# Seven block products for eight in a feed-forward of two inputs, and a modulation that is computed earlier

## The chip, the cores and the metric

The kernel runs on one core of a Trainium2 chip. The metric is the device time of one execution in microseconds, the median of several runs. Everything is float32 at the outside; the large matmuls run as three products of operands that are split in a rounded high part and a low remainder.

## What is computed

`x` is a sequence of 256 tokens of 1024 channels, `ctx` a context of 256 tokens. A first block (mixer and feed-forward) runs on `x`; then come two layers on `x` and `ctx` together, whose shifts, scales and gates come from a modulation, a matrix product of a condition vector. Cut to what the change touches:

```python
def swiglu(h, w_in, w_out):
    g, u = jnp.split(h @ w_in, 2, axis=-1)
    return (jax.nn.silu(g) * u) @ w_out

for l in range(2):
    with_ctx = l < 1
    mod = (silu_c @ w_mod[l] + b_mod[l])[:, None, :]
    mod_c = (silu_cc @ w_mod[l] + b_mod[l])[None, None, :]
    ...
    y, yc = even_mixer(h, hc, ...) if l % 2 == 0 else odd_mixer(h, hc, ...)
    x = x + gt_m * rmsnorm(y, g_post_mix[l])
    h = modulate(x, g_pre_ffn[l], sh_f, sc_f)
    x = x + gt_f * rmsnorm(swiglu(h, w_ffn_in[l], w_ffn_out[l]), g_post_ffn[l])
    if with_ctx:
        ctx = ctx + cgt_m * rmsnorm(yc, g_post_mix[l])
        hc = modulate(ctx, g_pre_ffn[l], csh_f, csc_f)
        ctx = ctx + cgt_f * rmsnorm(swiglu(hc, w_ffn_in[l], w_ffn_out[l]), g_post_ffn[l])
```

The hidden width is 2816, 22 blocks of 128. Only layer 0 has a feed-forward of both inputs.

## The kernel before

**Stages.** One program runs straight through, by the profiled execution: the first block's mixer (0 to 345 us), its feed-forward (345 to 566), layer 0's mixing (566 to 701), a boundary and block 0 of the feed-forward (701 to 728), layer 0's feed-forward (to 1030), layer 1's attention (to 1260) and its feed-forward (to 1457).

**Weights.** `wraw` (L173) loads a raw weight tile over the SP queue, in one of 3 buffers of 128x1024 ("m", 512 KB) or 4 of 128x512 ("f", 256 KB). `wload` (L178) splits it with `split` (L313): ScalarE rounds the high part (L314), VectorE subtracts for the low one (L315). `prod_w1` (L208) multiplies 128 weight columns with an input of 256 tokens: for each of 8 pieces of the 1024 channels three matmuls, high by high, high by low, low by high (L215 to L217). `mm_x` (L226, L227 to L229) is the same with tokens as the stationary side.

**Feed-forward.** `ffn_main` (L419) goes over 22 hidden blocks. With a second input (`more`, the context in `ch`, `cl`) a block has 4 products of 24 matmuls of 128x256: gate and up of each input, 96 in all. `swiglu` (L413) needs a tanh on ScalarE and two operations on VectorE per input. The latent's hidden block is split and goes one block later through `Down.step` (L290), 12 matmuls of 128x512; the context's is kept in `hid` for a later stage.

**Boundary.** `boundary` (L390) closes a stage: it adds the result to `x`, normalizes two tiles of 128 tokens (`rstd_of` L318, whose power runs on GpSimd, L331), transposes them (L346) and splits them. Between the two tiles `fill` may put other matmuls; ahead of layer 0's feed-forward that is `ctx_first` (L1266), gate and up of the context for block 0.

**Modulation.** `modulation(l, ...)` (L501) is a generator: three parts `b` of two halves `h` of eight raw tiles `wraw` of 512 KB. A raw goes either through TensorE, four float32 matmuls against `sst` (`rows`, L528), or through VectorE into an accumulator, two operations a raw (L548, L550), which at the end of a half are picked into rows by TensorE. Layer 0's modulation runs in the first block. Layer 1's is started with layer 0's feed-forward: its first half on TensorE, the other five on VectorE.

**Order.** A generator handed to `side.start` is stepped whenever `tick` has gathered so many estimated microseconds of matmul work; `side.finish` runs it to its end. Within these hints a scheduler sets the final order of each engine's instructions. An engine and a queue work their list strictly in that order. The context's projections and attention (`ctx_project`, L1202) are such a side work of the first block's feed-forward; `down_f` (L1177) multiplies the context's attention result `cah`, `cal` with the output matrix in 96 matmuls of 128x512, and its place in the order is the scheduler's.

## Time and profile before

| what | value |
|---|---|
| median of 3 runs | 1454.36 us (1453.89 to 1455.94) |
| the profiled execution | 1459.17 us, its span 1457.4 us |
| mean granted clock of TensorE | 0.978 of full speed |
| TensorE busy | 1393.5 us, 96% |
| VectorE busy | 982.7 us, 67% |
| ScalarE busy | 717.7 us, 49% |
| GpSimd busy | 37.8 us, 3% |

Busy is the union of an engine's instructions. Matmuls overlap: a matmul's duration holds its way through the array, so what one costs in a row of them is the distance from start to start. A wait's releaser is inferred. PE is TensorE, DVE is VectorE, ACT is ScalarE, POOL is GpSimd, SP is the engine that issues most transfers.

### The profile page before, as it was taken

How to read it: one execution, taken by the hardware profiler on the slowest of the kernel's cores; microseconds unless marked ns; L12 is line 12 of the kernel's file. 1: busy time of each engine (PE TensorE's matmuls, PEld its weight loads, DVE VectorE, ACT ScalarE, POOL GpSimd, SP SyncE). 2: the span in 40 equal slices, each digit the busy share in tenths (PEclk: the TensorE clock that was granted, in tenths of full speed). 3: DMA queues.
4: the chain of work that ended last, by engine and by line, in shares of the span. 5: the costliest groups of instructions: out<-in, count | busy, mean ns of one | idle time of the engine just before them, and what ended most of it. 6: DMA issues, size and time to landing. Idle time of an engine off the chain costs nothing.

```text
span 1457.4 us, 25376 instructions
## 1 busy us (share of the span) xinstructions
PE 1393.5 (96%) x9900; PEld 1233.2 (85%) x9900; DVE 982.7 (67%) x1949; ACT 717.7 (49%) x1326; POOL 37.8 (3%) x58
## 2 busy tenths in 40 slices
PE   6999999999999998989899999999899999899997
PEld 5887879978999986877699999999778866799997
DVE  4877954576667656776686768664688886455555
ACT  4467743455554545557523232222577676344443
POOL 1000000000000000001000000000000000000000
PEclk8999999999999999989999999999999999899999
DMA  7763799857566552622875656543374511256663
GB/s 249 226 183 88 227 281 281 240 166 218 171 181 197 164 151 81 206 94 67 248 224 178 211 169 200 182 145 102 104 229 150 176 45 30 73 160 188 189 187 117
DMA packets 294464, 246.87 MB, mean 169 GB/s; under 512 B 11380, under 2 KB 273144, under 8 KB 294344
## 3 DMA queue, kind: packets, MB, share of 16 engines
q1 hardware_dynamic: 294344, 245.25, 55.1%
q8 instruction: 78, 1.28, 0.4%
q14 instruction: 42, 0.34, 0.1%
HBM read 244.13 MB, written 1.08 MB: 168 GB/s over the span
## 4 chain that ended last, share of the span: by engine, by line
PE 82%; DVE 7%; ACT 4%; DMA 3%; issue 2%; POOL 1%; SPq 0%; POOLq 0%; DVEq 0%; ACTq 0%
PE pb L215 14%; PE pb L216 14%; PE pb L217 14%; PE pb L227 9%; PE pb L228 9%; PE pb L229 9%; PE pb L1052 2%; PE pb L528 2%; PE pb L1004 2%; PE pb L1046 1%; DVE mlo L315 1%; DMA mraw<-in_w_in_dram 1%; ACT mhi L314 1%; DMA wraw<-in_w_mod_dram 1%; PE pb L772 1%
## 5 line engine op out<-in xcount | busy, mean ns | idle before, releaser
L315 DVE TENSOR_TENSOR mlo<-mraw,mhi 128x1024 fp32r<-128x1024 f32 (+2 forms) x297 | 360.8, 1218 | 279.1 <-ACT mhi L314 269.8
L314 ACT ACTIVATE mhi<-mraw 128x1024 fp32r<-128x1024 f32 (+2 forms) x297 | 311.8, 1054 | 426.7 <-PE pb L216 227.5
L215 PE MATMUL pb<-xTh,mhi 128*128 128x256 f32 x1632 | 466.2, 286 | 1.2 <-DVE ge L861 0.7
L217 PE MATMUL pb<-xTh,mlo 128*128 128x256 f32 x1632 | 464.3, 285 | 1.3 <-DVE mlo L315 1.3
L216 PE MATMUL pb<-xTl,mhi 128*128 128x256 f32 x1632 | 464.8, 285 | 0.0
L215 PEld LDWEIGHTS pb<-xTh,mhi 128*128 128x128 f32 x1632 | 314.0, 192 | 12.2 <-issue 6.1
L217 PEld LDWEIGHTS pb<-xTh,mlo 128*128 128x128 f32 x1632 | 314.0, 192 | 3.9 <-DVE mlo L315 2.0
L216 PEld LDWEIGHTS pb<-xTl,mhi 128*128 128x128 f32 x1632 | 314.2, 193 | 3.4 <-DVE xTl L315 0.8
L227 PE MATMUL pb<-mhi,fh 128*128 128x512 f32 x264 | 104.2, 395 | 0.0
L228 PE MATMUL pb<-mlo,fh 128*128 128x512 f32 x264 | 103.7, 393 | 0.0
L229 PE MATMUL pb<-mhi,fl 128*128 128x512 f32 x264 | 103.0, 390 | 0.0
L550 DVE SCALAR_TENSOR_TENSOR acc<-wraw,sst,acc 128x1024 f32<-128x1024 f32 x70 | 86.9, 1280 | 6.0 <-DMA wraw<-in_w_mod_dram 5.6
L227 PE MATMUL pb<-mhi,xTh 128*128 128x256 f32 (+1 forms) x272 | 81.0, 298 | 4.1 <-ACT xTh L314 2.5
L228 PE MATMUL pb<-mlo,xTh 128*128 128x256 f32 (+1 forms) x272 | 81.4, 299 | 1.8 <-DVE mlo L315 1.8
L229 PE MATMUL pb<-mhi,xTl 128*128 128x256 f32 (+1 forms) x272 | 80.9, 297 | 0.4 <-DVE xTl L315 0.4
L315 DVE TENSOR_TENSOR flo<-fraw,fhi 128x512 fp32r<-128x512 f32 x88 | 59.9, 688 | 12.6 <-ACT fhi L314 10.7
L314 ACT ACTIVATE fhi<-fraw 128x512 fp32r<-128x512 f32 x88 | 54.5, 625 | 17.7 <-PE pb L229 9.2
L227 PEld LDWEIGHTS pb<-mhi,xTh 128*128 128x128 f32 x272 | 54.3, 200 | 7.6 <-ACT xTh L314 2.9
L229 PEld LDWEIGHTS pb<-mhi,fl 128*128 128x128 f32 x264 | 49.6, 188 | 10.8 <-DVE fl L315 0.3
L228 PEld LDWEIGHTS pb<-mlo,xTh 128*128 128x128 f32 x272 | 54.4, 200 | 4.9 <-DVE mlo L315 2.6
L227 PEld LDWEIGHTS pb<-mhi,fh 128*128 128x128 f32 x264 | 49.8, 189 | 10.1 <-issue 0.8
L228 PEld LDWEIGHTS pb<-mlo,fh 128*128 128x128 f32 x264 | 49.8, 189 | 8.8 <-issue 0.8
(402 smaller groups left out, 2339.2 us busy)
## 6 DMA issues: line engine op xcount, KB each, us to landing
...
```

The costliest lines, as they stand in the source:

```text
L215: nc.tensor.matmul(dst, wh, xh[:, k], start=(k == 0), stop=False)
L216: nc.tensor.matmul(dst, wh, xl[:, k], start=False, stop=False)
L217: ins = nc.tensor.matmul(dst, wl, xh[:, k], start=False, stop=(k == 7))
L227: nc.tensor.matmul(dst, xh_k, wh, start=first, stop=False)
L228: nc.tensor.matmul(dst, xh_k, wl, start=False, stop=False)
L229: return nc.tensor.matmul(dst, xl_k, wh, start=False, stop=last)
L314: return (nc.scalar.activation(hi, src, AF.Copy), nc.vector.tensor_sub(lo, src, hi.bitcast(F32)))
L315: nc.vector.tensor_sub(lo, src, hi.bitcast(F32)))
L528: ins = nc.tensor.matmul(pb[32 * q:32 * q + 32, h * 256:(h + 1) * 256], lhs, rhs[:, q], start=first, stop=last, tile_position=(0, 32 * q), ...
L550: ins = nc.vector.scalar_tensor_tensor(acc[:, r_], raw, col, acc[:, r_], OP.mult, OP.add)
L1004: nc.tensor.matmul(sb[j][:, n * S:(n + 1) * S], qs[a][hd, i * P:(i + 1) * P], keys[n][b][hd, kv, :], start=(m == 0), stop=(m == 2))
L1052: nc.tensor.matmul(ob[64 * j:64 * j + 64, :S], vals[k // 2](k % 2, kv), pts[j][:, k], start=(k == 0), stop=(k == 2 * nb - 1), skip_group_c ...
```

## The change

**The products.** In blocks 1 to 21 of layer 0's feed-forward the gate matrix and the up matrix are taken as halves by input channel (`g0`, `g1`, `u0`, `u1`, each 4 pieces of 128x128) and the two inputs likewise (`x0`, `x1` and the context's). The four results, gate and up of both inputs, come from seven half products of 12 matmuls of 128x256, 84 for 96. For this GpSimd makes four sums of 128x512 of the raw weights per block (`s1`, `s2`, `u0` in place, `s4`); each of the seven halves is split by itself; ScalarE copies one product out of PSUM (`e1`) and VectorE makes five sums of products. The sums take slots of the "f" raw pool. Sums of the inputs (`t1` to `t4`) are made once around the boundary by `sums_of_inputs`, partly on GpSimd. Block 0 stays as it was.

**The modulation of layer 1.** Part `b` = 0 runs wholly on VectorE beside the first block's feed-forward, as a second side work (`side2`) that starts once the context's projections have begun. Parts 1 and 2 run wholly on TensorE during layer 0's mixing: 32 raws in pairs, with two buffers (`nraw` 2, `step` 2), all done before layer 0's feed-forward. In the feed-forward itself nothing of it is left.

```diff
...
+        lo, hi = slice(0, 4), slice(4, 8)
+        f = lambda a: a.bitcast(F32)
+        t3 = mp.tile([P, 4, S], F32, tag="mP", name="t3", bufs=2)
+        nc.vector.tensor_sub(t3, f(ch[:, hi]), f(ch[:, lo]))
+        u = mp.tile([P, 4, S], F32, tag="mP", name="u3", bufs=2)
+        nc.vector.tensor_sub(u, f(cl[:, hi]), f(cl[:, lo]))
+        nc.vector.tensor_add(t3, t3, u)
+        split(*rooms[2], t3)
+        yield
+        t2 = t3
+        nc.vector.tensor_add(t2, t3, keep[0])
+        split(*rooms[1], t2)
+        nc.gpsimd.tensor_tensor(u, f(ch[:, lo]), keep[0], op=OP.subtract)
+        nc.gpsimd.tensor_tensor(u, u, f(cl[:, lo]), op=OP.add)
+        nc.gpsimd.tensor_tensor(keep[1], keep[1], t2, op=OP.subtract)
+        split(*rooms[0], u)
+        h4, l4 = rooms[3]
+        nc.scalar.activation(h4, keep[1], AF.Copy)
+        for j in range(2):
+            js = slice(2 * j, 2 * j + 2)
+            nc.vector.tensor_sub(l4[j], keep[1][:, js], h4[:, js].bitcast(F32))
...
+            def halves(s, *src):
+                hi = wpool[s].tile([P, CH[s]], F32R, tag=s + "hi", name=s + "hi", bufs=HLB[s])
+                lo = wpool[s].tile([P, CH[s]], F32R, tag=s + "lo", name=s + "lo", bufs=HLB[s])
+                res = []
+                for j, a in enumerate(src):
+                    o = slice(512 * j, 512 * j + 512)
+                    split(hi[:, o], lo[:, o], a)
+                    res.append(parts(hi[:, o].rearrange("p (a b) -> p a b", a=4),
+                                     lo[:, o].rearrange("p (a b) -> p a b", a=4)))
+                return res
+            def product(dst, w, b, fresh=True):
+                for k in range(4):
+                    (wh, wl), (bh, bl) = w[k], b[k]
+                    nc.tensor.matmul(dst, wh, bh, start=fresh and k == 0, stop=False, skip_group_check=True)
+                    nc.tensor.matmul(dst, wh, bl, start=False, stop=False, skip_group_check=True)
+                    nc.tensor.matmul(dst, wl, bh, start=False, stop=(k == 3), skip_group_check=True)
+            def swiglu2(t, g, u):
+                nc.scalar.activation(t, g, AF.Tanh, scale=0.5)
+                nc.vector.scalar_tensor_tensor(t, t, 1.0, g, OP.add, OP.mult)
+                nc.vector.tensor_mul(t, t, u)
...
+            for c in range(1, 22):
+                tick(9.1)
+                g = wraw(wview(W, 0, 8, c * P, P), 8, P, "m")
+                u = wraw(wview(W, 0, 8, 2816 + c * P, P), 8, P, "m")
+                g0, g1, u0, u1 = g[:, :512], g[:, 512:], u[:, :512], u[:, 512:]
+                s1, s2, s4 = [wpool["f"].tile([P, 512], F32, tag="fraw", name="fs", bufs=RAWB["f"])
+                              for j in range(3)]
+                nc.gpsimd.tensor_tensor(s1, u0, u1, op=OP.add)
+                nc.gpsimd.tensor_tensor(s2, s1, g0, op=OP.subtract)
+                nc.gpsimd.tensor_tensor(u0, g0, u0, op=OP.subtract)
+                nc.gpsimd.tensor_tensor(s4, g1, s2, op=OP.subtract)
+                b1, b2, b3 = [bank("MF"[(c + j) % 2])[:, :S] for j in range(3)]
+                wg0, ws2 = halves("m", g0, s2)
+                product(b1, wg0, x0)
+                product(b2, ws2, t2)
+                e1 = fp.tile([P, S], F32, tag="e1", name="e1", bufs=2)
+                nc.scalar.activation(e1, b1, AF.Copy)
+                e2 = fp.tile([P, S], F32, tag="e2", name="e2")
+                nc.vector.tensor_add(e2, b2, e1)
+                ws3, wg1 = halves("m", u0, g1)
+                product(b3, ws3, t3)
+                product(b1, wg1, x1, False)
+                ws1, = halves("f", s1)
+                product(b2, ws1, t1, False)
+                e4 = fp.tile([P, S], F32, tag="e4", name="e4")
+                nc.vector.tensor_add(e4, b2, e1)
+                nc.vector.tensor_add(e4, b3, e4)
+                dn.step(*prev)
+                wu1, = halves("f", u1)
+                product(b3, wu1, t4, False)
+                ws4, = halves("f", s4)
+                product(b2, ws4, c1, False)
+                nc.vector.tensor_add(e2, b3, e2)
+                nc.vector.tensor_add(e1, b2, e1)
+                t = fp.tile([P, S], F32, tag="ft", name="ft", bufs=2)
+                swiglu2(t, b1, e2)
+                prev = hidden(c, t)
+                swiglu2(hid[:, c], e1, e4)
...
+                if not vec:
+                    for k in range(0, 8, step):
+                        if step < 8:
+                            raws = [load(k + j) for j in range(step)]
+                            yield
+                        pb = bank("F")
+                        for j in range(step):
+                            rows(sst[:, k + j], raws[j] if step < 8 else load(k + j), j == 0, j == step - 1)
+                            if step == 8:
+                                yield
+                        add()
...
+    def second(acc):
+        while not begun:
+            yield
+        yield from modulation(1, wm, mods[1], acc, (0,))
+    side2.start(second(lambda: cp.tile([P, 2, 4, 256], F32, tag="ftmp", name="acc")), 6)
...
+    wm1 = ExitStack()
+    side.start(modulation(1, wm1.enter_context(tc.tile_pool(name="wm1", bufs=1, side="right")), mods[1],
+                          None, (1, 2), 2, 2), 4)
...
+    more = sums_of_inputs(ch, cl, keep, rooms, mp)
+    next(more)
+    xh, xl = boundary(dn.y, 1.0, gain_row(Gm, "gm0"), Af, Bf, fill=ctx_first, keep=keep)
+    rooms[1] = pair(*[ap_.tile([P, D], F32R, tag="mtmp", name="t2p", bufs=2) for j in range(2)])
+    rooms[3] = (pair(ap_.tile([P, D], F32R, tag="mG", name="t4h", bufs=1))[0],
+                [cst.tile([P, 2, S], F32R, tag="mmod", name="t4l", bufs=2) for j in range(2)])
+    next(more)
+    side.finish()
     l0.close()
+    wm1.close()
...
-    side.start(modulation(1, wm1.enter_context(tc.tile_pool(name="wm1", bufs=1, side="right")), mods[1],
-                          lambda: cp.tile([P, 2, 4, 256], F32, tag="ftmp", name="acc")), 5)
-    y = ffn_main(xh, xl, T["w_ffn_in_2"][0], 0, T["w_ffn_in_2"][0], 2816, T["w_ffn_out_2"][0],
-                 (ch, cl, hid), first)
+    y = ffn_pair(xh, xl, ch, cl, rooms, T["w_ffn_in_2"][0], T["w_ffn_out_2"][0], first, hid)
...
```

**What moves in the order.** TensorE, the boundary at the start of layer 0's mixing, while the first tile is normalized; `cah` is the context's attention result, `wraw` a raw of the modulation, `xn` the normalized tile. Before:

```order
L1052 MATMUL pb_6539<-PTm_6525,kvc_3895 64x256
L1052 MATMUL pb_6539<-PTm_6532,kvc_3895 64x256
L227 MATMUL pb_7497<-fhi_7501,cah_5646 128x512 [waits PE_49]
L228 MATMUL pb_7497<-flo_7502,cah_5646 128x512
L229 MATMUL pb_7497<-fhi_7501,cal_5647 128x512
L227 MATMUL pb_7497<-fhi_7513,cah_5646 128x512
```

After:

```order
L1202 MATMUL pb_6655<-PTm_6648,kvc_3901 64x256
L668 MATMUL pb_6896<-wraw_6809,sst_179 32x256 [waits DMAHW3_49,DMAHW4_49,DMAHW2_49,DMAHW5_49,DMAHW1_49,DMAHW7_49,DMAHW0_49,PE_49]
L668 MATMUL pb_6896<-wraw_6809,sst_179 32x256 x3
L668 MATMUL pb_6896<-wraw_6811,sst_179 32x256 [waits DMAHW4_49]
L668 MATMUL pb_6896<-wraw_6811,sst_179 32x256 x3
L668 MATMUL pb_6970<-wraw_6906,sst_179 32x256 [waits DMAHW5_49,DVE_49]
L351 MATMUL pb_6732<-tab_76,xn_6711 128x128 [waits DVE_49]
L351 MATMUL pb_6732<-tab_76,xn_6711 128x128 x3
L351 MATMUL pb_6744<-tab_76,xn_6711 128x128 x4
L668 MATMUL pb_6970<-wraw_6906,sst_179 32x256 x3
L668 MATMUL pb_6970<-wraw_6908,sst_179 32x256 [waits DMAHW6_49]
```

The context's down matmuls have left this place (they now stand from the last part of the layer's attention on); six raws of the modulation stand there, with DMA waits of their own, four of them behind or between the transposes.

TensorE, the end of layer 0's mixing; `a0h`, `a0l` is the attention result, `xTh` by `mhi` is `ctx_first`. Before:

```order
L228 MATMUL pb_7795<-mlo_7901,a0h_7124 128x512
L229 MATMUL pb_7795<-mhi_7900,a0l_7125 128x512
L215 MATMUL pb_7989<-xTh_7727,mhi_7992 128x256 [waits DVE_49,Activation_49]
L216 MATMUL pb_7989<-xTl_7728,mhi_7992 128x256 [waits DVE_49]
L217 MATMUL pb_7989<-xTh_7727,mlo_7993 128x256 [waits DVE_49]
L215 MATMUL pb_7989<-xTh_7727,mhi_7992 128x256
```

After:

```order
L233 MATMUL pb_8091<-mhi_8266,a0l_7330 128x512
L668 MATMUL pb_8092<-wraw_7784,sst_179 32x256 [waits DMAHW6_49,Activation_49]
L668 MATMUL pb_8092<-wraw_7784,sst_179 32x256 x3
L668 MATMUL pb_8092<-wraw_7786,sst_179 32x256 [waits DMAHW7_49]
L668 MATMUL pb_8092<-wraw_7786,sst_179 32x256 x3
L351 MATMUL pb_8338<-tab_76,xn_8317 128x128 [waits DVE_49]
L351 MATMUL pb_8338<-tab_76,xn_8317 128x128 x3
L351 MATMUL pb_8349<-tab_76,xn_8317 128x128 x4
L668 MATMUL pb_8142<-wraw_8102,sst_179 32x256 [waits DMAHW0_49,PE_49]
L668 MATMUL pb_8142<-wraw_8102,sst_179 32x256 x3
```

After the last down matmul two raws follow, the first tile's transposes, and then more raws (seven, in all nine ahead of `ctx_first`); before, `ctx_first` followed at once.

VectorE, one hidden block of layer 0's feed-forward. Before:

```order
L315 TENSOR_TENSOR mlo_11194<-mraw_11191,mhi_11193 128x1024 [waits DMAHW0_49,PE_49,Activation_49]
L416 SCALAR_TENSOR_TENSOR ft_11106<-ft_11106,pb_10996 128x256 [waits Activation_49]
L417 TENSOR_TENSOR ft_11106<-ft_11106,pb_10996 128x256 [waits DVE_49]
L315 TENSOR_TENSOR mlo_11259<-mraw_11256,mhi_11258 128x1024 [waits DMAHW1_49,Activation_49]
L315 TENSOR_TENSOR fl_11114<-ft_11106,fh_11113 128x256 [waits Activation_49]
L315 TENSOR_TENSOR mlo_11267<-mraw_11264,mhi_11266 128x1024 [waits DMAHW2_49,PE_49,Activation_49]
```

After (`mlo` and `flo` of 128x512 are the low parts of weight halves, `fs` a sum, `e1`, `e2`, `e4` sums of products; the last line of this piece is the split of the second up half):

```order
L319 TENSOR_TENSOR mlo_10995<-mraw_10980,mhi_10994 128x512 [waits DMAHW7_49,Activation_49]
L319 TENSOR_TENSOR mlo_10995<-fs_10985,mhi_10994 128x512 [waits Activation_49]
L319 TENSOR_TENSOR mlo_11029<-mraw_10982,mhi_11028 128x512 [waits DMAHW0_49,PE_49,Activation_49]
L535 SCALAR_TENSOR_TENSOR ft_10969<-ft_10969,pb_10831 128x256 [waits Activation_49]
L572 TENSOR_TENSOR e4_10914<-pb_10832,e1_10864 128x256 [waits DVE_49,PE_49]
L319 TENSOR_TENSOR mlo_11029<-mraw_10980,mhi_11028 128x512 [waits Activation_49]
L573 TENSOR_TENSOR e4_10914<-pb_10833,e4_10914 128x256 [waits DVE_49]
L319 TENSOR_TENSOR flo_11059<-fs_10984,fhi_11058 128x512 [waits Activation_49]
L319 TENSOR_TENSOR mlo_11080<-mraw_11077,mhi_11079 128x1024 [waits DMAHW1_49,Activation_49]
L579 TENSOR_TENSOR e2_10866<-pb_10833,e2_10866 128x256 [waits PE_49]
L319 TENSOR_TENSOR flo_11096<-mraw_10982,fhi_11095 128x512 [waits Activation_49]
L580 TENSOR_TENSOR e1_10864<-pb_10832,e1_10864 128x256 [waits PE_49]
```

Weight splits went from one tile of 1024 at a time to halves, with the sums of products between them. The raw tile read by the last line here is the up tile, whose buffer the next block's up load takes.

GpSimd, the four sums of one block, of which there were none:

```order
L554 TENSOR_TENSOR fs_10984<-mraw_10982 128x512 [waits DMAHW0_49,DVE_49]
L555 TENSOR_TENSOR fs_10985<-fs_10984,mraw_10980 128x512 [waits DMAHW7_49,DVE_49,Pool_49]
L556 TENSOR_TENSOR mraw_10982<-mraw_10980,mraw_10982 128x512 [waits DMAHW6_49,DVE_49]
L557 TENSOR_TENSOR fs_10986<-mraw_10980,fs_10985 128x512 [waits Pool_49]
```

The first waits for the up tile's load, the second for the gate tile's as well; the third writes over a half of the up tile.

## Rows read from the trace of the kernel before

**Rows 1.** Part 1 of the page: busy time, share of the span, instructions of TensorE.

```profile
PE 1393.5 (96%) x9900; PEld 1233.2 (85%) x9900; DVE 982.7 (67%) x1949; ACT 717.7 (49%) x1326; POOL 37.8 (3%) x58
```

**Rows 2.** Part 4 of the page: the chain that ended last, shares by engine.

```profile
PE 82%; DVE 7%; ACT 4%; DMA 3%; issue 2%; POOL 1%; SPq 0%; POOLq 0%; DVEq 0%; ACTq 0%
```

**Rows 3.** Windows: three stages; busy us (instructions) of each engine, granted clock, DMA share, GB/s.

```profile
345.00:560.00 215.00, 214.11 (x1523) 197.04 (x1522) 140.86 (x249) 113.45 (x199) 5.40 (x5) 1.00 0.60 180
566.30:700.80 134.50, 122.43 (x738) 98.61 (x738) 99.57 (x235) 84.00 (x175) 10.51 (x13) 0.94 0.39 121
740.00:1030.00 290.00, 290.00 (x2242) 276.41 (x2241) 194.69 (x242) 83.81 (x126) 1.06 (x2) 1.00 0.57 175
```

**Rows 4.** Timeline of ScalarE: start us, us; a tanh of two neighbouring blocks.

```profile
838.25 0.38 ACT L415 ACTIVATE hid<-pb 128x256 f32<-128x256 f32 x1 [1.89 <-PE pb L217]
852.50 0.38 ACT L415 ACTIVATE hid<-pb 128x256 f32<-128x256 f32 x1 [1.89 <-PE pb L217]
```

**Rows 5.** Timeline of TensorE: two neighbouring matmuls of each width.

```profile
689.62 0.39 PE L229 MATMUL pb<-mhi,a0l 128*128 128x512 f32 x1
689.85 0.39 PE L227 MATMUL pb<-mhi,a0h 128*128 128x512 f32 x1
...
707.95 0.28 PE L217 MATMUL pb<-xTh,mlo 128*128 128x256 f32 x1
708.07 0.28 PE L215 MATMUL pb<-xTh,mhi 128*128 128x256 f32 x1
```

**Rows 6.** The chain from 740 to 1030 us: the first of five such pieces.

```profile
766.94 1.00 PE pb L528 x16
```

**Rows 7.** Groups of VectorE by form, 740 to 1030 us: busy, mean ns, idle before.

```profile
L550 DVE SCALAR_TENSOR_TENSOR acc<-wraw,sst,acc 128x1024 f32<-128x1024 f32 x64 | 79.5, 1279 | 5.5 <-DMA wraw<-in_w_mod_dram 5.2
L315 DVE TENSOR_TENSOR mlo<-mraw,mhi 128x1024 fp32r<-128x1024 f32 x60 | 73.2, 1223 | 75.3 <-ACT mhi L314 70.0 <-PE pb L528 5.2
L417 DVE TENSOR_TENSOR hid<-hid,pb 128x256 f32<-128x256 f32 x20 | 8.4, 418 | 0.5
```

**Rows 8.** Part 5 of the page: the splits of 128x512.

```profile
L315 DVE TENSOR_TENSOR flo<-fraw,fhi 128x512 fp32r<-128x512 f32 x88 | 59.9, 688 | 12.6 <-ACT fhi L314 10.7
L314 ACT ACTIVATE fhi<-fraw 128x512 fp32r<-128x512 f32 x88 | 54.5, 625 | 17.7 <-PE pb L229 9.2
```

**Rows 9.** Groups of TensorE by form, 566.3 to 590 us: the first of three alike.

```profile
L227 PE MATMUL pb<-fhi,cah 128*128 128x512 f32 x14 | 5.8, 414 | 0.0
```

**Rows 10.** Timeline of SP: a weight load's issue.

```profile
866.16 0.37 SPq L175 DMA_DIRECT2D mraw<-in_w_ffn_in_dram  x1
```

**Rows 11.** Windows of half a microsecond: the slice where that load's last bytes move.

```profile
869.00:869.50 0.50, 0.50 (x6) 0.40 (x4) 0.00 (x0) 0.00 (x0) 0.00 (x0) 1.00 0.52 154
```

**Rows 12.** The chain from 700 to 728 us: its two longest waits.

```profile
705.56 6.04 DMA wraw<-in_w_mod_dram
...
712.34 4.87 DMA wraw<-in_w_mod_dram
```

**Rows 13.** Timeline: the mixing's last down matmul (TensorE), block 0's second tanh (ScalarE).

```profile
700.55 0.39 PE L229 MATMUL pb<-mhi,a0l 128*128 128x512 f32 x1
...
727.59 0.36 ACT L415 ACTIVATE ft<-pb 128x256 f32<-128x256 f32 x1
```

**Rows 14.** Timeline of GpSimd: a memset of 128x512.

```profile
0.73 0.53 POOL L507 MEMSET gp<- 128x512 f32 x1 [0.29 <-POOLq L1377]
```

**Rows 15.** Timeline of VectorE and GpSimd: GpSimd's power beside VectorE, at two places.

```profile
43.52 1.22 DVE L315 TENSOR_TENSOR mlo<-mraw,mhi 128x1024 fp32r<-128x1024 f32 x1
...
43.76 1.39 POOL L331 TENSOR_TENSOR rs<-ms,mhalf 128x1 f32<-128x1 f32 x1 [1.82 <-DVE ms L329]
...
44.66 0.28 DVE L499 TENSOR_TENSOR pidx<-rp,rp 128x128 f32<-128x128 f32 x1
...
1112.80 0.68 DVE L315 TENSOR_TENSOR flo<-fraw,fhi 128x512 fp32r<-128x512 f32 x1
...
1112.96 0.93 POOL L331 TENSOR_TENSOR rs<-ms,mhalf 128x1 f32<-128x1 f32 x1 [2.87 <-DVE ms L329]
```

118 lines of the change are left out of this document (80 added, 38 removed).

## The prediction

> **What bounds the kernel now.** I read the page's shares first: TensorE is busy 96% of the span [rows 1], and the chain that ended last runs over it for 82% [rows 2]. A matmul that is taken away therefore saves its time only where nothing else becomes late, so I read the stages one by one [rows 3]. In layer 0's feed-forward (740 to 1030 us) TensorE is busy in every microsecond while VectorE works 67% of them: this stage is bound by matmuls alone. In the first block's feed-forward (345 to 560) it is the same with 214 of 215 us. Layer 0's mixing, from 566.3 to 700.8 us, is the loose stage: TensorE idles 134.5 - 122.4 = 12.1 us there. The change takes from the first of these stages and gives to the other two.
>
> **The block of layer 0's feed-forward.** Two neighbouring blocks stand 852.50 - 838.25 = 14.25 us apart [rows 4]. That agrees with a count: 96 matmuls of 256 columns at a pitch of 0.12 us and 12 of 512 at 0.23 [rows 5], 96 x 0.119 + 12 x 0.2275 = 14.2. After the change 84 of the 96 remain: 84 x 0.119 + 2.73 = 12.73. If TensorE stayed the bound, 21 blocks would give back 21 x (14.26 - 12.73) = 32 us. Block 0 stays direct.
>
> It need not stay the bound. Per block VectorE now has seven weight halves of 512 to split, one of 1024, and ten operations of 256 (five new sums, four of the two SwiGLUs, one hidden split). By their durations [rows 7, 8] and since one that is queued starts about 0.08 us before the last one ends (43.52 + 1.22 against 44.66, [rows 15]), that is 7 x 0.61 + 1.14 + 10 x 0.335 = 8.8 us. That alone fits in 12.73. But GpSimd gets four sums of 128x512 per block, of loaded weights, and the trace has no such operation. Let P be its price. From below: a memset of that tile, which writes it and reads nothing, took 0.53 us [rows 14]. From above: two reads and a write, each as dear as that memset, 1.6 us. I take 1.1, the middle, for the sums have one more input than an operation that copies.
>
> Nor do GpSimd and VectorE run freely side by side. Where GpSimd's one-column power started behind a VectorE operation with two inputs from SBUF, it ended 0.41 us after that operation's end, both times, though it had started 0.24 and 0.16 us behind its start (43.76 + 1.39 against 43.52 + 1.22; 1112.96 + 0.93 against 1112.80 + 0.68) [rows 15]. So the two take turns. What a long GpSimd operation does to VectorE the trace doesn't show, and I take it as symmetric. VectorE and GpSimd then need 8.8 + 4P per block: 13.2 us for P = 1.1, 10.9 for 0.53, 15.2 for 1.6.
>
> The order gives a second bound, a loop. The load of the next block's up weights waits on SP for VectorE's split of this block's second up half. Its bytes have landed about 3.2 us after its issue (866.16, the last bytes in 869.0 to 869.5) [rows 10, 11]. Then GpSimd makes s1 and s2 (2P), ScalarE rounds s2 (0.62) [rows 8], and VectorE works through ten entries up to the next second up half: five halves, the 1024 tile and four of 256, 5 x 0.61 + 1.14 + 4 x 0.335 = 5.5. With 0.3 for hand-offs, an allowance, that is 9.65 + 2P, and 9.65 + 3P if one of GpSimd's other two sums falls into VectorE's stretch: 12.95 for P = 1.1, 14.45 for 1.6, 11.2 for 0.53. The longer bound decides: a block takes T = 13.2 us, and 21 blocks save 21 x (14.26 - 13.2) = **22 us**. The ends are 32 us saved (P up to 0.98, where 8.8 + 4P reaches 12.73) and 20 us lost (P = 1.6).
>
> The Trainium skill, "SBUF — State Buffer", section "🔬 SBUF: two separate sides", states that VectorE and GpSimd share a port pair by an exclusive lock: a VectorE operation with two SBUF inputs and a GpSimd operation that reads SBUF block each other wholly. By that rule VectorE's five new sums, which read PSUM, would not be shut out, and the bound by turns would fall to 10.1 us at P = 1.1; the loop alone would then hold, T = 12.95 and 5 us more saved. The pow rows [rows 15] agree with the lock. The skill's "GPSIMD Engine Reference", section "3.1 Elementwise — side-by-side cycle accounting", has 4497 ns for a sum of 2048 elements; a quarter, as an estimate 1.12 us, would give T = 13.3 and a sum 2 us worse. No run here shows it.
>
> **Modulation leaves this stage.** Five groups that fold VectorE's accumulators into rows stood on the path, each 1.00 us for its 16 records [rows 6]: **-5 us**. The accumulator work on VectorE, 64 operations [rows 7], was hidden beside matmuls and gives nothing back.
>
> **First block's feed-forward.** A third of the modulation comes here: 32 accumulator steps at 1.22 us are 39 us for VectorE, which has 140.9 of 215 [rows 3, 7]. They can start only once the context's projections have begun, in the last 145 us or so, and bring VectorE there to some 92%. TensorE gets two pick groups and transposes, 2.6 us. VectorE's splits will sometimes be late for TensorE: I take **+5**, between +2 (only the matmuls) and +10 (a sixth of the added VectorE work on the path besides).
>
> **Layer 0's mixing.** The other two thirds run on TensorE: 32 raw loads of 512 KB, 22 of them before the last Down matmul. One raw is 8 records, half of such a group of 16, so 0.5 us [rows 6]: 11 us. They would fit into the 12.1 idle us, but they also push out what fills a hole. Before, 3 x 14 matmuls of context-down stood between 566.3 and 590, while the boundary's norm was on the way [rows 9], 42 x 0.2275 = 9.6 us; the 54 others stood further on between the stage's own products. In the order after, all 96 stand in and behind the last part of the attention, and in the hole stand three pairs of raws, which wait for DMA with two buffers. A raw's load waits on SP for the matmul of the raw two before it, then needs 3.2 us, so the pairs cannot fill at TensorE's pace, and weight loads queue behind them on SP. 96 x 0.2275 = 22 us of filler go; I count 15 of it as new idle time (9.6 in the boundary's hole less 3 for the pairs there, and 8 to 9 of the later 12). 11 + 15 = **+26**; from +18 (the pairs fill half of it) to +33 (all of it).
>
> **Boundary and block 0.** Before, ctx_first followed the last Down at once, and block 0 ended at 727.59, 26.8 us after 700.8 [rows 13], itself late by two DMA waits for raws, of 6.04 and 4.87 us in the chain [rows 12]. After, four pairs and a half must pass TensorE before ctx_first: each buffer turns in 3.2 + 0.5 = 3.7 us, so from the first pair, already loaded, four turns: 0.5 + 4 x 3.7 = 15.3 us. Then ctx_first and x's products, 48 matmuls each (5.7 us), three more raws and what the transposes and DMA leave open, some 5 to 7 us: 33 to 35 us, **+7**; from +3 to +12. On GpSimd block 1's four sums, which wait for its weights, stand ahead of the second tile's power; that is inside the upper end.
>
> **The sum.** +5 + 26 + 7 - 5 - 22 = +11 us. The profiled execution took 1459.2 (span 1457.4), so a profile of after should read about 1470; against the median of 1454.36 it is **1465 us**.
>
> **Rivals.** *Faster: the raws fill the holes.* Place: the mixing. If the loads come early enough that the pairs run where TensorE idles, the stage grows by some 5 us, not 26: 5 + 5 + 7 - 27 = -10, **1444 us**. It decides at a growth of 15, where the sum is zero. For it speaks that 12.1 us idle and 121 GB/s leave room for 11 MB; against it, two buffers and the filler gone. *Much slower: GpSimd's sums are dear.* Above P = 1.37, 8.8 + 4P passes 14.26 and the seven products save nothing. At 1.45, T is 14.3 between loop and turns: 5 + 26 + 7 - 5 + 1 = +34, **1488 us**. The pow rows speak for taking turns; nothing shows P. *No change: TensorE stays the bound* (P below 0.98, or the turns don't hold) with the mixing as I sum it: 5 + 26 + 7 - 5 - 32 = +1, **1455 us**. This is also where "seven for eight" does all that it says and the moved modulation eats it.
>
> **How the numbers follow.** Forecast 0.38, filled holes 0.24, dear sums 0.22, TensorE bound 0.16. Within 0.2% (2.9 us, about what a measurement of this kernel tells from no change) lie half of the last case and the edges of its neighbours: 0.12. Faster: the filled holes and the good side of the last case, 0.27. Slower: the rest, 0.61. The range leaves out the outer parts of the two far cases: 1443 to 1490, and the forecast's own range, mostly the mixing's ends, is 1457 to 1474.
>
> **What would show it.** Two blocks' tanh rows in layer 0's feed-forward stand T apart: 12.7 means TensorE bound, 13.2 as summed, 14.3 or more dear sums; TensorE's idle time there names its releaser, and GpSimd's rows give P. The time from the last down matmul of the first block to that of the mixing is 134.5 before; 160 is my step, 140 the faster rival. From there to block 0's second tanh 34 us, with TensorE waiting for DMA on modulation rows. I am wrong in kind if VectorE's two-input rows run undisturbed beside GpSimd's sums, or if TensorE's idle time in the mixing isn't ahead of modulation or boundary rows.

## The result and the profile after

The changed kernel took 1521.02 us (median of 4 runs, 1516.93 to 1524.89) against 1454.12 for the kernel before: a ratio of 1.046, 95% interval 1.044 to 1.048, 67 us slower. The forecast was 1465 with a range from 1443 to 1490: the sign was right, the size was not, by 56 us.

Parts 1 and 4 of the page of the changed kernel: busy time by engine, and the chain that ended last.

```profile
PE 1394.1 (92%) x9792; PEld 1212.1 (80%) x9792; DVE 1068.8 (70%) x2138; ACT 774.4 (51%) x1456; POOL 171.8 (11%) x146
...
PE 59%; DVE 13%; DMA 12%; POOL 6%; issue 5%; ACT 5%; POOLq 0%; SPq 0%; DVEq 0%; ACTq 0%
```

TensorE is as busy as before [rows 1], in a span 66 us longer, and the chain that went over it for 82% [rows 2] now goes over it for 59%, with DMA, VectorE and GpSimd behind it. The time was not added as work but as waiting. The windows of the changed kernel (busy us and instructions of PE, PEld, DVE, ACT, POOL, then granted clock, DMA share, GB/s): the first block's feed-forward, the mixing, the boundary with block 0, and a stretch of layer 0's feed-forward.

```profile
345.00:560.00 215.00, 211.45 (x1527) 193.75 (x1526) 171.09 (x277) 111.99 (x194) 8.26 (x8) 1.00 0.70 213
574.00:739.20 165.20, 142.05 (x901) 104.94 (x900) 102.86 (x240) 83.46 (x172) 11.24 (x12) 0.91 0.47 146
739.20:790.30 51.10, 30.38 (x224) 21.10 (x224) 39.01 (x55) 21.67 (x42) 16.13 (x10) 0.70 0.40 124
900.00:1000.00 100.00, 89.32 (x656) 83.47 (x655) 78.14 (x126) 45.33 (x83) 39.08 (x28) 1.00 0.37 112
```

To be compared with [rows 3]. In layer 0's feed-forward TensorE was busy all the time; now it idles 10.7 of 100 us. The mixing idles 165.2 - 142.1 = 23.1 us, where it was 12.1, and is 19.6 us busier; the boundary idles 20.7 of 51.1 us, at a granted clock of 0.70.

The two profiled executions, cut at the same places. The first block's feed-forward runs from its first to its last down matmul, the mixing from there to its own last down matmul, the boundary from there to block 0's tanh for the latent [rows 13], the feed-forward from there to the later tanh of its last block:

| stage, us | before | after | moved | predicted |
|---|---|---|---|---|
| first block's mixer (not edited) | 346.4 | 348.6 | +2.2 | 0 |
| first block's feed-forward | 219.8 | 225.4 | +5.6 | +5 |
| layer 0's mixing | 134.6 | 165.1 | +30.5 | +26 |
| boundary and block 0 | 26.8 | 51.1 | +24.3 | +7 |
| layer 0's feed-forward, blocks 1 to 21 | 301.5 | 304.6 | +3.1 | -27 |
| the rest | 428.3 | 428.2 | -0.1 | 0 |
| span | 1457.4 | 1523.1 | +65.7 | +11 |

The mixer's 2.2 us are the spread of a stage without an edit: among all runs here its end lies between 341.4 and 348.6, and the rest, from the end of layer 0's feed-forward on, takes 423.0 to 428.3. So the runs below are compared by stages and not by spans. Two terms failed: 30 us in the feed-forward, 17 in the boundary.

**The feed-forward.** Timeline of ScalarE, the context's tanh of two neighbouring blocks of the changed kernel, for [rows 4]:

```profile
893.45 0.41 ACT L534 ACTIVATE hid<-e 128x256 f32<-128x256 f32 x1
...
907.89 0.41 ACT L534 ACTIVATE hid<-e 128x256 f32<-128x256 f32 x1
```

14.44 us apart, and over the stage 304.6 / 21 = 14.5: a block is as long as before, though TensorE has 12 matmuls less in it. The chain through one block of the changed kernel, in order of time (start us, us, what) shows why:

```profile
891.53 4.43 DMA mraw<-in_w_ffn_in_dram
...
896.13 1.26 POOL fs L554
...
897.47 1.62 POOL fs L555
899.09 1.26 POOL mraw L556
...
900.37 0.64 ACT mhi L318
...
901.04 0.31 DVE mlo L319
901.35 1.17 issue
902.52 0.41 DVE ft L535
...
904.79 1.15 DVE mlo L319
...
905.96 5.11 DMA mraw<-in_w_ffn_in_dram
```

It is a loop, with one turn from 891.53 to 905.96, 14.43 us. The up weights land (4.43 us after their issue, 5.11 in the next turn), GpSimd makes s1, s2 and the sum in `u0` one behind the other (1.26, 1.62, 1.26), ScalarE rounds, VectorE splits and sums, and its split of the down tile (904.79) is what the next up load waits for. TensorE is nowhere in it.

VectorE and GpSimd lock each other out inside it. Timeline of the changed kernel, the two engines side by side:

```profile
896.10 1.29 POOL L554 TENSOR_TENSOR fs<-mraw 128x512 f32<-128x512 f32 x1 [8.47 <-DMA mraw<-in_w_ffn_in_dram]
...
896.46 1.48 DVE L319 TENSOR_TENSOR mlo<-mraw,mhi 128x512 fp32r<-128x512 f32 x1
...
900.30 1.75 POOL L557 TENSOR_TENSOR fs<-mraw,fs 128x512 f32<-128x512 f32 x1
```

VectorE's split of 128x512 that starts 0.36 us behind the first sum takes 1.48 us where it took 0.69 [rows 8]; it ends at 897.94, 0.55 us after the sum, which ends at 897.39. The second sum, started at 897.47 while that split runs (the chain above has it), takes 1.62 for 1.29. The fourth sum (900.30 to 902.05) holds up the split that starts at 901.04 in the chain.

**The mixing and the boundary.** Group of TensorE's modulation matmuls by form in the changed kernel's mixing (count, busy us, mean ns, idle before and its releaser):

```profile
L668 PE MATMUL pb<-wraw,sst 128*32 128x256 f32 x160 | 18.5, 467 | 11.6 <-DMA wraw<-in_w_mod_dram 11.6
```

160 records are 20 raws: 18.5 us busy, 0.93 a raw, and 11.6 us of waits for their loads, in all 30.1 us beside the 30.5 that the stage grew. Where in the stage it grew is another matter. The layer's attention ends at 680.98 before and at 694.89 in the changed kernel, 114.7 and 120.9 us into the mixing, so up to there it is only 6 us late. Windows from there to the last down matmul, before and changed:

```profile
681.00:700.80 19.80, 19.30 (x91) 15.24 (x92) 14.04 (x26) 11.44 (x20) 3.01 (x5) 1.00 0.64 191
694.90:739.20 44.30, 42.51 (x190) 33.65 (x190) 26.88 (x47) 25.18 (x45) 3.68 (x5) 1.00 0.38 114
```

Here the stage loses 24 us, with TensorE at work nearly throughout. 78 of the context's 96 down matmuls stand in this part now (78 x 0.2275 = 17.7 us by [rows 5]), where before all 96 were done earlier, and 22 of the stage's own down matmuls more than before. The raws and their waits have taken the places that these had. The boundary on TensorE's timeline, from the last down matmul on:

```profile
740.14 1.07 PE L668 MATMUL pb<-wraw,sst 128*32 128x256 f32 x16 [0.81 <-ACT mod L363]
...
747.02 1.08 PE L668 MATMUL pb<-wraw,sst 128*32 128x256 f32 x8 [1.79 <-DMA wraw<-in_w_mod_dram]
748.42 1.08 PE L668 MATMUL pb<-wraw,sst 128*32 128x256 f32 x8 [0.32 <-DMA wraw<-in_w_mod_dram]
751.84 1.08 PE L668 MATMUL pb<-wraw,sst 128*32 128x256 f32 x8 [2.34 <-DMA wraw<-in_w_mod_dram]
754.61 1.08 PE L668 MATMUL pb<-wraw,sst 128*32 128x256 f32 x8 [1.69 <-DMA wraw<-in_w_mod_dram]
757.51 1.08 PE L668 MATMUL pb<-wraw,sst 128*32 128x256 f32 x8 [1.82 <-DMA wraw<-in_w_mod_dram]
760.28 1.08 PE L668 MATMUL pb<-wraw,sst 128*32 128x256 f32 x8 [1.69 <-DMA wraw<-in_w_mod_dram]
763.13 1.08 PE L668 MATMUL pb<-wraw,sst 128*32 128x256 f32 x8 [1.77 <-DVE flo L319]
764.14 0.58 PE L219 MATMUL pb<-xTh,mhi 128*128 128x256 f32 x1
...
777.15 0.38 PE L529 MATMUL pb<-xTh,mhi 128*128 128x256 f32 x1 [0.72 <-ACT modT L717]
781.59 0.58 PE L220 MATMUL pb<-xTl,mhi 128*128 128x256 f32 x1 [4.06 <-DVE xTl L319]
```

Eight records are a raw. From 747.02 to 763.13 seven raws pass, 2.7 us apart, and each takes 1.08 us. Only then, 24.9 us after the last down matmul, comes `ctx_first` (764.14, L219). The product of `x` that starts at 777.15 waits till 781.59 for a split.

### The profile page after: what moved, and what is told of

The parts are those of the page before. It is cut to its first block, busy times and chain, and to the rows that moved or that the text cites. A ratio compares the mean times of both kernels' runs of the same rounds, so it can differ in the third digit from the quotient of the medians.

```text
span 1523.1 us, 25762 instructions
## 1 busy us (share of the span) xinstructions
PE 1394.1 (92%) x9792; PEld 1212.1 (80%) x9792; DVE 1068.8 (70%) x2138; ACT 774.4 (51%) x1456; POOL 171.8 (11%) x146
## 3 DMA queue, kind: packets, MB, share of 16 engines
q8 instruction: 77, 1.26, 0.3%
HBM read 244.15 MB, written 1.08 MB: 161 GB/s over the span
## 4 chain that ended last, share of the span: by engine, by line
PE 59%; DVE 13%; DMA 12%; POOL 6%; issue 5%; ACT 5%; POOLq 0%; SPq 0%; DVEq 0%; ACTq 0%
PE pb L219 8%; PE pb L220 8%; PE pb L221 8%; PE pb L231 7%; PE pb L232 7%; PE pb L233 7%; DMA mraw<-in_w_ffn_in_dram 5%; DVE mlo L319 3%; PE pb L668 2%; PE pb L1202 2%; DMA wraw<-in_w_mod_dram 2%; POOL fs L555 2%; ACT mhi L318 2%; POOL fs L554 2%; POOL mraw L556 1%
## 5 line engine op out<-in xcount | busy, mean ns | idle before, releaser
L319 DVE TENSOR_TENSOR mlo<-mraw,mhi 128x1024 fp32r<-128x1024 f32 (+3 forms) x318 | 382.3, 1205 | 184.7 <-ACT mhi L318 177.8
L318 ACT ACTIVATE mhi<-mraw 128x1024 fp32r<-128x1024 f32 (+3 forms) x318 | 307.1, 969 | 314.1 <-PE pb L220 144.5
L220 PE MATMUL pb<-xTl,mhi 128*128 128x256 f32 x960 | 276.5, 288 | 4.1 <-DVE xTl L319 4.1
L219 PE MATMUL pb<-xTh,mhi 128*128 128x256 f32 x960 | 278.0, 290 | 0.1
L221 PE MATMUL pb<-xTh,mlo 128*128 128x256 f32 x960 | 275.4, 287 | 0.0
L219 PEld LDWEIGHTS pb<-xTh,mhi 128*128 128x128 f32 x960 | 187.1, 195 | 9.9 <-issue 5.7
L220 PEld LDWEIGHTS pb<-xTl,mhi 128*128 128x128 f32 x960 | 187.1, 195 | 7.0 <-DVE xTl L319 4.3
L221 PEld LDWEIGHTS pb<-xTh,mlo 128*128 128x128 f32 x960 | 187.0, 195 | 2.1 <-DVE mlo L319 1.2
L335 POOL TENSOR_TENSOR rs<-ms,mhalf 128x1 f32<-128x1 f32 x36 | 24.1, 669 | 719.3 <-DVE ms L333 719.3
L668 PE MATMUL pb<-wraw,sst 128*32 128x256 f32 x640 | 59.9, 434 | 24.9 <-DMA wraw<-in_w_mod_dram 22.3
L233 PEld LDWEIGHTS pb<-mhi,fl 128*128 128x128 f32 x264 | 49.6, 188 | 10.7 <-DVE fl L319 0.2
```

Of the source, the lines that this page charges most:

```text
L219: nc.tensor.matmul(dst, wh, xh[:, k], start=(k == 0), stop=False)
L220: nc.tensor.matmul(dst, wh, xl[:, k], start=False, stop=False)
L221: ins = nc.tensor.matmul(dst, wl, xh[:, k], start=False, stop=(k == 7))
L233: return nc.tensor.matmul(dst, xl_k, wh, start=False, stop=last)
L318: return (nc.scalar.activation(hi, src, AF.Copy), nc.vector.tensor_sub(lo, src, hi.bitcast(F32)))
L319: nc.vector.tensor_sub(lo, src, hi.bitcast(F32)))
```

## The experiments

All are cut from the changed kernel. `e1` to `e9` are single runs beside one run of the kernel before (1454 to 1457 us), except e8, which was timed. The stages are those of the table above, in us: ffn 1 is the first block's feed-forward, ffn 0 that of layer 0.

| run | ffn 1 | mixing | boundary | ffn 0 | span |
|---|---|---|---|---|---|
| before | 219.8 | 134.6 | 26.8 | 301.5 | 1457.4 |
| changed | 225.4 | 165.1 | 51.1 | 304.6 | 1523.1 |
| e1 up weights in own buffers | 225.5 | 164.2 | 48.0 | 282.8 | 1492.3 |
| e2 sums of weights left out | 225.4 | 164.6 | 48.1 | 269.9 | 1477.5 |
| e3 sums of weights on VectorE | 225.2 | 163.8 | 51.7 | 270.2 | 1481.6 |
| e4 old products | 225.1 | 163.2 | 46.3 | 294.0 | 1502.9 |
| e5 as e3, three raw buffers | 225.5 | 158.4 | 45.0 | 274.4 | 1474.2 |
| e6 as e3, raws in the feed-forward | 225.4 | 135.1 | 39.2 | 329.2 | 1497.7 |
| e7 as e6, sums of inputs on VectorE | 225.4 | 135.3 | 35.7 | 331.2 | 1499.9 |
| e8 as e7, raws spread | 230.3 | 133.8 | 35.4 | 294.4 | 1465.4 |
| e9 as e8, all raws there | 219.8 | 134.3 | 35.5 | 310.0 | 1467.0 |

**e1: is it the loop or the turns?** The up tile gets two buffers of its own; the three that it shared with the gate and the down tile stay with these two.

```diff
-                u = wraw(wview(W, 0, 8, 2816 + c * P, P), 8, P, "m")
+                u = fp.tile([P, 1024], F32, tag="ur", name="ur", bufs=2)
+                nc.sync.dma_start(u.rearrange("p (a b) -> p a b", a=8), wview(W, 0, 8, 2816 + c * P, P))
```

> The changed kernel, with the up weights of blocks 1 to 21 in two buffers of their own, so that their load no longer waits for a split of the block before. Changed kernel: hidden blocks stand 14.47 us apart, one profile at 1523 us span. Theory A (the loop: up load, two sums on GpSimd, rounding, splits of one block, next up load) says the distance falls to TensorE's own 12.7 to 13.0 us, 21 blocks give 30 to 37 us, the span is about 1488 to 1493 us. Theory B (VectorE and GpSimd take turns and together are the bound, 8.8 us of VectorE and four sums at 1.3 us) says 14.0 us at least, span 1513 to 1523 us.

It took 1494.12 us. Timeline of ScalarE in e1, the context's tanh of two neighbouring blocks, then a window of the same stage:

```profile
902.23 0.42 ACT L534 ACTIVATE hid<-e 128x256 f32<-128x256 f32 x1 [1.47 <-DVE e L581]
...
915.06 0.42 ACT L534 ACTIVATE hid<-e 128x256 f32<-128x256 f32 x1 [0.79 <-DVE e L581]
```

```profile
900.00:1000.00 100.00, 99.22 (x741) 94.21 (x740) 88.70 (x142) 49.96 (x94) 51.80 (x31) 1.00 0.40 122
```

12.83 us apart (13.0 in the mean of the middle blocks) and TensorE busy 99.2 of 100 us: theory A. The stage as a whole took 282.8, not the 270 that 21 such blocks make, since its first blocks are longer (782.90 to 810.04 for the first of these distances). In these first 26.9 us VectorE is busy 23.7, GpSimd 19.9 and TensorE 18.9, at a granted clock of 0.75; what holds them up was not followed further. GpSimd's four sums stayed, at 1.26 us or more each, and so did VectorE's 8.8 us of work per block; 8.8 + 4 x 1.26 = 13.8 us do not fit in 12.83 or 13.0 if the two take turns with everything. That theory, on which the prediction's 13.2 stood, is refuted. What takes turns is narrower. Timeline of e1, GpSimd's last two sums of a block and three operations of VectorE beside them:

```profile
897.33 1.75 POOL L557 TENSOR_TENSOR ur<-mraw,ur 128x512 f32<-128x512 f32 x1
899.04 2.27 POOL L558 TENSOR_TENSOR fs<-mraw,fs 128x512 f32<-128x512 f32 x1
...
898.48 1.68 DVE L319 TENSOR_TENSOR mlo<-mraw,mhi 128x1024 fp32r<-128x1024 f32 x1 [0.56 <-ACT mhi L318]
900.08 0.41 DVE L580 TENSOR_TENSOR e<-pb,e 128x256 f32<-128x256 f32 x1
900.42 1.45 DVE L319 TENSOR_TENSOR flo<-ur,fhi 128x512 fp32r<-128x512 f32 x1
```

The split of 128x1024 at 898.48 (two inputs from SBUF) meets the sum that began at 897.33 and takes 1.68 us for 1.21; it ends at 900.16. The last sum, begun at 899.04, waits for that and then runs to 901.31, 2.27 us for 1.26. The operation at 900.08, which makes `e2` and reads `pb` from PSUM, lies inside that and takes 0.41 as ever, as all such operations beside a sum do in this stage (75 of them, 0.41 to 0.42). The split at 900.42, of 128x512 from SBUF, is held up till 901.31 again and takes 1.45 for 0.69. This is what the Trainium skill states on "SBUF — State Buffer", section "🔬 SBUF: two separate sides": the exclusive lock is between a VectorE operation with two SBUF inputs and a GpSimd operation that reads SBUF. The trace agrees; the prediction set that narrower reading aside for the broader one.

**e2 and e3: what do GpSimd's sums cost, and could VectorE make them?** In e2 the four sums of weights are left out and raw halves take their place; in e3 they stand on VectorE.

```diff
-                nc.gpsimd.tensor_tensor(s1, u0, u1, op=OP.add)
+                nc.vector.tensor_tensor(s1, u0, u1, op=OP.add)
...
```

> The changed kernel, with the four sums of weights per block left out: the raw halves are used in their place, so the output is not the reference's; number, sizes and order of matmuls, splits and loads stay. Theory A (loop) and theory B (turns) both lose GpSimd's 5 us per block: distance of hidden blocks 12.7 to 12.9 us (TensorE alone), span about 1487 to 1490 us. Rival C (the bunched weight loads, three of 512 KB at a time, are late by themselves): the distance stays above 13.5 us, span above 1503 us. The boundary ahead of the stage keeps its 51 us.

> The changed kernel, with the four sums of weights per block on VectorE. VectorE then has 8.8 + 4 x 0.61 = 11.2 us per block, below TensorE's 12.7. Theory A (loop): the loop keeps the up load of 5 us and has two sums of 0.6 instead of 1.3 to 1.6 in it, so it shortens by about 1.6 us and all waits for GpSimd go: distance 12.7 to 13.2, span 1487 to 1497 us. Theory B (turns): 12.7 as well. If it stays at 14.4 both fall and the load itself is the bound.

They took 1479.3 and 1483.42 us, with the stage at 269.9 and 270.2, which is 21 blocks of 12.86 in the mean. A window of e3:

```profile
900.00:1000.00 100.00, 99.56 (x749) 94.64 (x748) 87.01 (x169) 51.60 (x93) 0.00 (x0) 1.00 0.42 127
```

TensorE is busy 99.6 of 100 us and VectorE 87.0 with all sums on it. So once the sums are out of the loop or cheap in it, the stage gives back 301.5 - 270.2 = 31 us. By e4 below 7.5 of it are the modulation's, which leaves 24 for the seven products (some 26 by the distance of the middle blocks, 14.26 in e4 and 13.0 here), where the count of matmuls says 32. Rival C, that the bunched loads are late by themselves, is refuted: e2 has the same loads.

**e4: is the boundary late by the raws or by the sums of the inputs?** Old products, no sums, and the boundary's call as in the kernel before; the modulation as in the change.

```diff
-    y = ffn_pair(xh, xl, ch, cl, rooms, T["w_ffn_in_2"][0], T["w_ffn_out_2"][0], first, hid)
+    y = ffn_main(xh, xl, T["w_ffn_in_2"][0], 0, T["w_ffn_in_2"][0], 2816, T["w_ffn_out_2"][0],
+                 (ch, cl, hid), first)
...
-    more = sums_of_inputs(ch, cl, keep, rooms, mp)
```

> The changed kernel with the old direct products in layer 0's feed-forward (four of 24 matmuls per block) and without the sums of the inputs; the modulation stays where the change put it. Distance of hidden blocks 14.26 us, the stage 300 us where the changed kernel takes 305. Theory A (the modulation's raws, each late by its load, hold up ctx_first and so the boundary): from the mixing's last down matmul to block 0's second tanh still 38 to 43 us (26.8 before, 51.1 changed), span 1505 to 1511 us. Rival (the sums of the inputs on GpSimd and VectorE hold up the boundary): 27 to 31 us, span 1494 to 1499 us. The mixing keeps its 165 us in both.

1504.7 us; the boundary takes 46.3, against 51.1 with the sums. Waits of TensorE around it in e4:

```profile
PE pb L668 <- DMA wraw<-in_w_mod_dram: 9.7, 6, 2.3
```

Without any sums 19.5 of the 24.3 us stay: the raws. The other 4.8 need not be the sums of the inputs alone. With these but without block 1's sums of weights e2 is at 48.1, and e1, which has both, at 48.0; so single runs leave the inputs' share at 2 to 5 us. The expectation's 38 to 43 was still too low. The feed-forward took 294.0, 7.5 us less than before, all of it the modulation's: e4's blocks stand 14.26 us apart, as those before do that have no piece of it, while those with one stand up to 15.91 apart. Against e4 the changed kernel's products cost 304.6 - 294.0 = 10.6 us.

**e5: is it the raws' loads?** As e3, with a third buffer for the raws.

```diff
-                          None, (1, 2), 2, 2), 4)
+                          None, (1, 2), 3, 2), 4)
```

> As e3 (sums of weights on VectorE), and the modulation's raws in the mixing have three buffers for two. e3: mixing 163.8 us, boundary and block 0 51.7. Theory A (each raw is late by its own load, since its buffer is free only after a matmul two raws before): a third load in flight takes away a third or more of the DMA waits, 11.6 us in the mixing and 9.6 in the boundary; mixing 156 to 161, boundary 44 to 48, span 1469 to 1477 us. Rival (the raws' matmuls themselves, at the clock they get behind a wait, and the missing filler are the price): mixing and boundary together stay within 4 us of e3, span 1478 to 1484.

1475.92 us: mixing 158.4 for 163.8 and boundary 45.0 for 51.7, 12 us together, as theory A said. The rest of the price stays: the raws' own matmuls, the loads that are still late, and the context's down matmuls at their later place.

**e6 and e7: the modulation's place.** As e3, parts 1 and 2 are started with layer 0's feed-forward, on TensorE; e7 has the sums of the inputs on VectorE as well.

```diff
+    side.start(modulation(1, wm1.enter_context(tc.tile_pool(name="wm1", bufs=1, side="right")), mods[1],
+                          None, (1, 2), 2, 2), 9)
     y = ffn_pair(xh, xl, ch, cl, rooms, T["w_ffn_in_2"][0], T["w_ffn_out_2"][0], first, hid)
```

> As e3 (sums of weights on VectorE), with parts 1 and 2 of the modulation on TensorE during layer 0's feed-forward, 32 raws of about 0.5 us spread over 21 blocks, for the mixing and the boundary. Theory A (the modulation's place is the price): mixing back to 134 to 137 us, boundary and block 0 30 to 37 (26.8 before, the sums of the inputs are new), feed-forward 270 + 16 to 20 = 286 to 290 us; span 1447 to 1457, that is at or below the kernel before (1457). Rival (the sums of the inputs, or the order the scheduler finds, keep the boundary long): boundary 42 us or more, span above 1460.

> As e6, with the three 128x1024 sums of the inputs on VectorE too, so that nothing but the norm's powers is left on GpSimd there. In the changed kernel these three stood at 775 to 785 us and VectorE's operations beside them took 3.3 us for 1.2. Theory (each holds VectorE up for as long as it lasts): the boundary is 3 to 6 us shorter than e6's, span likewise. Rival (VectorE is the longer queue there, and three more operations of 1.2 us just change places): within 1.5 us of e6.

1499.47 and 1501.71 us. The mixing is back to 135.1 and 135.3: all of its 30 us came with the raws. The context's down matmuls, which the prediction counted as a lost filler, came back with it. Lines of `cah` in the changed kernel and in e6, first and last start:

```profile
L231 PE MATMUL pb<-fhi,cah x32: 389/389/504, 682.1 to 712.4; 128*128 128x512 f32 x32
L231 PE MATMUL pb<-fhi,cah x32: 388/393/628, 582.8 to 670.4; 128*128 128x512 f32 x32
```

In e6 to e9 they start in the boundary's hole, as before. So no run here has the raws without the moved filler, or the moved filler without the raws, and what each costs by itself stays open. The boundary is at 39.2 and 35.7, so the sums of the inputs cost 3.5 less on VectorE than on GpSimd. But the feed-forward took 329 and 331, 59 more than e3 for 16 us of raws. A window of e6, its first 55 us:

```profile
745.00:800.00 55.00, 31.35 (x213) 17.05 (x214) 13.13 (x25) 5.85 (x13) 0.53 (x1) 0.66 0.65 206
```

TensorE works 31 of 55 us at a granted clock of 0.66: nine pairs of raws stand in the first block. The counter of the side work runs on while nothing is queued, and when the generator was started it had enough for many steps at once. It may have been my edit's fault and not the place's, which e8 tests.

**e8: spread.** The counter is cleared first, three buffers, one pair for about 13 us of matmuls.

```diff
+    side.due = 0.0
     side.start(modulation(1, wm1.enter_context(tc.tile_pool(name="wm1", bufs=1, side="right")), mods[1],
-                          None, (1, 2), 2, 2), 9)
+                          None, (1, 2), 3, 2), 13)
```

> As e7 (all sums on VectorE, the raws of parts 1 and 2 in layer 0's feed-forward), with one pair of raws per hidden block from the first on and three buffers; in e7 nine pairs stood in its first block, since the counter of the side work had run up before it was started, and the stage took 331 us. If bunching was e7's loss, the stage takes 270 + 32 x 0.5 + 2 = 286 to 292 us, with the mixing at 135 and the boundary at 36; span 1452 to 1460, within 0.4% of the kernel before on either side. If raws late by their loads cost as much one by one, 300 us or more and a span above 1468.

1463.98 us (5 runs, 1460.55 to 1467.75), a ratio to before of 1.0062 with an interval of 1.0037 to 1.0088. A window of e8's feed-forward and the longest wait of TensorE in its boundary:

```profile
780.00:850.00 70.00, 70.00 (x562) 63.79 (x561) 61.40 (x120) 34.43 (x61) 0.00 (x0) 1.00 0.62 194
...
PE pb L351 <- DVE xn L346: 9.2, 1, 9.2
```

In that stretch TensorE works all of 70 us, raws included; the stage takes 294.4, 2 us above what was expected. The edit changes three things at once (the counter, the third buffer, the step), and which of them ended e7's loss is not separated. 57 us of the change's 67 are gone. What is left against before is the boundary, +8.6, where the second tile's transposes wait 9.2 us for VectorE, whose list has sums of inputs and weights ahead of them, and the first block's feed-forward, +10.5 here: 5 us more than in the other runs with the same work there, with a wait of 2.8 us for ScalarE at 494 and a granted clock of 0.83 from 490 to 510 us, where the changed kernel keeps 1.00. This version is the best one found, and it is 0.6% slower than the kernel before.

**e9: part 0.** As e8, with part 0 as raws in layer 0's feed-forward too.

```diff
-    side2.start(second(lambda: cp.tile([P, 2, 4, 256], F32, tag="ftmp", name="acc")), 6)
...
-                          None, (1, 2), 3, 2), 13)
+                          None, (0, 1, 2), 3, 2), 9)
```

> As e8, with part 0 of the modulation too on TensorE in layer 0's feed-forward, for VectorE in the first block's feed-forward: 48 raws there, none elsewhere. From the first to the last down matmul of the first block's feed-forward it is 219.8 us before and 225.4 in the changed kernel. Theory (part 0's accumulator steps on VectorE make its splits late for TensorE): back to 219 to 221 us, while layer 0's feed-forward goes from 294 to 302 to 306. Rival (another order of the scheduler, not part 0): 224 us or more stays. Span 1463 to 1472 us either way.

1468.77 us. The first block's feed-forward is back to 219.8, the time before to a tenth, so part 0 and its place were the whole price. Its window in e9, for the first line of [rows 3] and of the changed kernel's windows:

```profile
345.00:560.00 215.00, 214.11 (x1519) 196.87 (x1518) 140.20 (x246) 111.98 (x196) 4.41 (x4) 1.00 0.58 178
```

VectorE is back at 140.2 us from 171.1 and TensorE at 214.1 from 211.5. Layer 0's feed-forward took 310.0, more than the 302 to 306 expected; why the added 16 raws cost 15.6 us and not 8 was not followed up.

## Why the prediction was wrong

- **First block's feed-forward, +5:** +5.6, and e9 takes it away whole: part 0 is the cause. How it costs that is only in part as named: of TensorE's 3.3 us of waits there, 0.5 end with a split on VectorE and 2.8 with ScalarE, and why ScalarE was late was not followed.
- **Mixing, +26:** +30.5, inside the term's bounds, but by luck in part: both halves are off, to opposite sides. The raws were priced at 0.5 us from a group that stood between other matmuls at full clock; behind waits, at a stage clock of 0.91, they took 0.93: 18.5 us for 11 (and 20 of them stood there, not 22). The new idle time was 11 us, not 15, and TensorE's waits for late raws are as long. The lost filler is neither shown nor refuted as a cause: that the stage loses its time behind the attention, where 17.7 us of filler now stand, speaks for it, and no run separates the two.
- **Boundary, +7:** +24.3, twice the upper bound. The step that failed is the turn of a buffer, 3.2 + 0.5 = 3.7 us: the chain below has a wait of 7.07 us for the first raw, beside which two weight loads had gone out, and waits of 5.00 and 4.49 where two loads are under way, and a raw's matmuls took 1.08 for 0.5, so a buffer's turn is 4.8 to 6.2 us (every second raw in the timeline above) and `ctx_first` starts after 24.9 us, not 15.3. That is 9.6 of the 17 us missed. A load that was alone on the queue [rows 10, 11] gave the price for two at a time. The row that knew better was at hand: [rows 12] has 4.87 and 6.04 for the same raws at the same place. And the sums of the inputs, set at nothing, cost 2 to 5 (e4). The chain of the changed kernel from 739 to 792 us, three of its waits:

```profile
741.30 7.07 DMA wraw<-in_w_mod_dram
...
749.56 5.00 DMA wraw<-in_w_mod_dram
...
755.75 4.49 DMA wraw<-in_w_mod_dram
```

And the timeline there, VectorE and GpSimd:

```profile
775.45 3.33 DVE L480 TENSOR_TENSOR t<-t,keep 128x1024 f32<-128x1024 f32 x1
778.70 3.43 DVE L319 TENSOR_TENSOR xTl<-keep,xTh 128x512 fp32r<-128x512 f32 x2
...
775.34 2.36 POOL L482 TENSOR_TENSOR u<-xTh,keep 128x1024 f32<-128x1024 f32 x1 [11.82 <-ACT keep L363]
777.78 3.21 POOL L483 TENSOR_TENSOR u<-u,xTl 128x1024 f32<-128x1024 f32 x1
```

VectorE's sum of 128x1024 takes 3.33 and two splits of 512 take 3.43 beside GpSimd's 2.36 and 3.21; e8's sum of that size on VectorE alone took 1.22.

- **Modulation out of the stage, -5:** right in kind and too small, for e4's stage is 7.5 us shorter than before.
- **The blocks, -22:** they cost 10.6 us instead (e4 against the change), for a block takes 14.5 us and not 13.2. This is the largest miss. The loop was named, and so were its parts: the load, two sums, the rounding, VectorE's row of splits. The step that failed is the loop's sum. Three terms were short. The load was 4.4 to 5.1 us, not 3.2, since gate, up and down loads go out within 3.4 us (903.92 to 907.31 on SP's timeline below). P is 1.29 us where nothing disturbs it, and the four sums take 1.32, 1.53, 1.32 and 1.74 in the mean, not 1.1. And three of GpSimd's sums stand in the loop, not two, with the fourth holding up VectorE's split of `u0` (901.04 to 902.52 in the chain, the 1.17 us of "issue" among it: 1.5 us for 0.6). Where the loop closes was misread too, in the order ahead of the prediction already: the up load goes out at 905.96, before the split of the up half has started (906.59, to 907.28), so it takes the buffer of the down tile, whose split stands two entries ahead of the up half's; it is the down load, at 907.31, that takes the up tile's. By the prediction's own formula P = 1.5 gives 9.65 + 4.5 = 14.15, near the 14.5 measured, but partly by luck: the load in it is 1.2 to 1.9 us short and the row of splits 0.9 too long. The other bound, turns of all operations, was refuted by e1. Its narrower form was also mis-summed: without the five new sums it is 13.2 - 5 x 0.335 = 11.5 us, not 10.1, which leaves the loop the longer one either way. The estimate from the Trainium skill's "GPSIMD Engine Reference", section "3.1 Elementwise — side-by-side cycle accounting", 1.12 us, stands against 1.29 measured.

SP's timeline in the changed kernel, one block (the first line is the gate and the up load):

```profile
903.92 2.40 SPq L179 DMA_DIRECT2D mraw<-in_w_ffn_in_dram  x2
907.31 0.34 SPq L179 DMA_DIRECT2D mraw<-in_w_ffn_out_dram  x1
```

- **The rivals.** "Dear sums", 1488 us, came nearest, by its effect. "The raws fill the holes" did not come: the mixing grew by 30.5 us and not by 5. "TensorE stays the bound" became true in the blocks of e1 and e3, but not in the change.
